# A hybrid attention and DeltaNet block: values in two half loads, and two delta heads' operands written in place

## The chip, the cores and the metric

The kernel runs on one core of a Trainium2 chip. The metric is the device time of one execution in microseconds (us), as a median over runs; every time in this document comes from such runs or from a profiled execution. Engines are named as the profile names them: PE is the matrix engine (TensorE), PEld its weight loads, DVE the vector engine, ACT the scalar engine, POOL the GpSimd engine, and SP the engine whose queue issues nearly all transfers of this kernel (SPq in the profile).

## The reference

One decoder block over 1024 tokens of width 1024, in float32. It normalises the input, projects it with one combined matrix, runs two groups of heads side by side, gates and normalises what they give, projects back, adds the input and normalises again:

```python
h = rmsnorm(x, norm1_w[layer])
proj = jnp.einsum('btd,de->bte', h, w_in[layer])
# stick-breaking attention: 8 heads of 64, query blocks of 128 rows over the causal keys
z = jnp.einsum('bhqd,bhkd->bhqk', qb, kb).astype(jnp.float32) * scale
sp = jnp.where(causal, jax.nn.softplus(z), 0.0)
tail = lax.cumsum(sp, axis=sp.ndim - 1, reverse=True) - sp
attn = jnp.where(causal, jnp.exp(jax.nn.log_sigmoid(z) - tail), 0.0)
outs.append(jnp.einsum('bhqk,bhkd->bhqd', attn.astype(v.dtype), vb))
# gated DeltaNet: 4 heads of 128, causal convolution of width 4 and silu on q, k, v, then
# chunks of tokens, a triangular solve in each, and a state carried from chunk to chunk
qkv = jax.nn.silu(causal_depthwise_conv(jnp.concatenate([g_q, g_k, g_v], axis=-1), gdn_conv_w[layer]))
v_new = u_c - jnp.einsum('bhcd,bhde->bhce', w_c, state)
o_c = jnp.einsum('bhcd,bhde->bhce', q_c * jnp.exp(g_c)[..., None], state) + jnp.einsum('bhij,bhje->bhie', a_c, v_new)
state = state * jnp.exp(g_last)[..., None, None] + jnp.einsum('bhcd,bhce->bhde', k_c * ..., v_new)
# both groups: rmsnorm per head, times silu of a gate, then
x = x + jnp.einsum('bte,ed->btd', mixed, w_out[layer])
return rmsnorm(x, final_norm_w)
```

## The kernel before, in words

Most products of the kernel are taken as three products of high and low parts (`mm3`), 128x512 at a time. The work on PE falls into three stretches. First the attention's queries and half of its values are projected. Then comes a long middle in which three kinds of work are interleaved: the remaining projections (`projections`, tile `pp`), attention (`attention`, `window`), and the delta heads (`delta_pre`, `delta_substitute`, `delta_solve`, `delta_scan`). The last stretch holds the products with the output matrix (`products_delta`, then `products_attention`; rows `pp<-wo` and `pp<-woh`), whose first factor `mm` is made for each block of 128 tokens from the heads' outputs and the gates.

The order of the work is not written down. While the program is built, a model of the engines (`Model`, `Recorder`) plays it through with costs written into the kernel: each stream is a generator, `interleave` takes the stream with the lowest number whose inputs are ready, and projections (number 100) fill PE when nothing else is ready. What the model found becomes the fixed order of every engine and of the SP queue. So an edit at one place can move instructions everywhere behind it. An engine or queue then keeps to its order: what stands first waits, and what is behind it waits with it. All instructions are recorded by one helper, which is why every row of the profile has the same line, and rows are told apart by their tiles.

**Attention.** A head's queries and keys (`q2`, `kh`, `kl`) are loaded from DRAM, and its values into `v2a`: 8 blocks of 128 tokens, 512 KB, one buffer. A head has four windows w of 256 queries. Each makes scores (`pz<-kh,q`, `pz<-kl,q`), passes them through ACT, DVE and POOL (`sg`, `cc`), transposes them (`pz<-step,st`), splits them (`ahl`), and multiplies the values with them (`po<-ahl,v2a`). In step j of window w the product reads blocks 2j-2 and 2j-1 of `v2a`. So blocks 4 to 7 are read in windows 2 and 3 alone, and blocks 0 to 3 for the last time in step 2 of window 3. `attention_values` loads the next head's values when the last window of the head before has ended (flag `e..3`); on the chip the load waits for the last product that reads the buffer.

**Delta heads.** `g_evac` turns a projected half (512 tokens) into q, k or v: convolution on ACT and DVE, then POOL multiplies `ac` by its sigmoid. For heads 0 and 1 (`TURNED` = 2) the result is stored to `g_s`, and `delta_load` loads keys and queries from there into `kq`, one of four slots, one for each unit (a head's half: head h, half g is unit 2h+g). Units 0 to 3 get the four slots; unit 4 waits for unit 0 to be done. `gdn_pre` transposes them (`pz<-step,kw`) and makes the triangular matrices (`pz<-kq`), `gdn_sub` and `gdn_inv` solve them, and `gdn_chain` carries the state through a unit's four chunks (`pc<-state,kq`, `pc<-xct,xinv`, `pz<-v,ak`, `pz<-state,kq`, `pz<-vr,ak`). At a unit's end the output is normalised, transposed and stored (`og_s<-akf`).

**The output's products** take blocks of 128 tokens in order, b = 0 to 7. Blocks 0 to 3 need unit 6 of the scan, blocks 4 to 7 unit 7; the first factor of a block goes into one of four slots `ak`, two of which units 6 and 7 hold until they are stored, so block 3 too waits for unit 7.

Of the kernel before, what the change touches and what calls it, by code (L numbers as in the profile page):

```python
# [134 lines left out]
class Fixed:  # L135
# [33 lines left out]
    def words(self, t, name):  # L169
        n = t.tensor.name  # L170
        return self.place(list(t.shape), F32R, name, self.at[n], self.ck.regions[n])


class Model:
# [304 lines left out]
def block(tc, xT_d, x_d, n1_d, wE_d, wQ_d, wC_d, conv_d, alog_d, dtb_d, mixw_d, wo_d, fnw_d, out_d):  # L479
# [4 lines left out]
    with ExitStack() as top:  # L484
# [139 lines left out]
        for tag, bufs in (("kh", 1), ("kl", 1), ("q2", 1), ("v2a", 1), ("sg2", 1), ("cc", 2), ("cc", 2), ("sg3", 1)):  # L624
            if tag[0] == "s":
                chl.append(fx.tile([P, 2, 520], F32R, "chl", tag))
            else:
                t = at_.tile([P, 1040 + (48 if tag == "kl" else 0)], F32R, tag=tag, bufs=bufs, name="chl")
                chl.append(t[:, 0:1040].rearrange("p (a e) -> p a e", a=2))
# [235 lines left out]
        def z_evac(i):  # L865
# [9 lines left out]

            return evac

        def g_evac(h, kind):
            wv = conv[:, 4 * kind + h, :]
            last = []  # L880

            def evac(pt, half):
                pre = gd.tile([P, 515], F32, tag="pre", bufs=2, name="pre")
                if half == 0:
                    V.memset(pre[:, 0:3], 0.0)
                else:
# [104 lines left out]
        def delta_load():  # L991
            yield lambda: "dec" in flags
            for h in range(GH):
                for g in range(2):
                    u = 2 * h + g
                    gst[h, g] = {}
                    half = "" if g else ".0"
                    yield lambda: u < 4 or f"c{u - 4}" in flags
                    if u > 3:
                        yield flags[f"c{u - 4}"]  # L1000
                    kq = fx.tile([P, 4, 2, P], F32, "kq", "kq")
                    ts = slice(512 * g, 512 * g + 512)
# [8 lines left out]
                    ck.hold(kq, kn, nkv)  # L1011
# [308 lines left out]
        def attention_values():  # L1320
            yield lambda: "v1" in flags and "dec" in flags
            for h in range(SBH):
                yield lambda: h == 0 or f"e{h - 1}3" in flags
                hd["v", h] = v2 = at_.tile([P, NB, P], F32R, tag="v2a", name="v2a")
                flags[f"va{h}"] = S.dma_start(v2.bitcast(F32), v_s[:, :, h].rearrange("b s u d -> s b (u d)").bitcast(F32))

        def window(h, w, tok):
            q2, kh, kl = hd[h]
# [29 lines left out]
            for j in range(w + 2):  # L1358
                if j <= w:
                    yield lambda: busy["al"] < 2  # L1360
                    busy["al"] += 1
                    blocks = [(s, i) for s in (2 * j, 2 * j + 1) for i in range(2) if s <= 2 * w + i]
                    n = len(blocks)
                    tp = pz()
                    yield from turned(tp, [st[:, i, s * P:(s + 1) * P] for s, i in blocks])
                    ahl = at_.tile([P, 2, 512], F32R, tag="ahl", bufs=2, name="ahl")
                    if n == 4:
                        halves = ahl.rearrange("p s (m t) -> p s m t", m=2)
                        ah, al = halves[:, :, 0, :], halves[:, :, 1, :]
                        src = tp.rearrange("p (s t) -> p s t", s=2)  # L1370
                    else:
                        ah, al = ahl[:, 0, 0:n * P], ahl[:, 1, 0:n * P]
                        src = tp[:, 0:n * P]
                    A.activation(ah, src, AF.Copy)
                    r = V.tensor_tensor(al, src, ah.bitcast(F32), ALU.subtract)
                    if j == w:
                        busy["T"] = 0
                        busy[tok] = 0
                    parts.append((ahl, r))
                    yield  # L1380
                if j == 0:
                    continue
                if j == 1:
                    yield lambda: busy["po"] == 0
                    busy["po"] = 1
                    ov = po()
                    yield from until(f"va{h}")
                    v2 = hd["v", h]
                ahl, r = parts[j - 1]
                ov2 = ov.rearrange("p (m t) -> p m t", m=2)  # L1390
                yield r
                for s in (2 * (j - 1), 2 * (j - 1) + 1):
                    i0 = 0 if s <= 2 * w else 1
                    c = slice(256 * (s % 2), 256 * (s % 2) + (1 if i0 else 2) * P)
                    if j <= w:
                        TE.matmul(ov, v2[:, s, :], ahl[:, s % 2, :], start=s == 0, stop=False)
                    else:
                        TE.matmul(ov2[:, :, i0 * P:256], v2[:, s, :], ahl[:, :, c], start=s == 0, stop=s == 2 * w + 1)
                busy["al"] -= 1
                if j < w + 1:  # L1400
                    yield
# [49 lines left out]
        def weight(k, wh, wl):  # L1451
            w = raws[k][0]
            A.activation(wh, w, AF.Copy, scale=mixw[:, k:k + 1])
            wts[k] = wh, wl, V.scalar_tensor_tensor(wl, w, mixw[:, k:k + 1], wh.bitcast(F32), ALU.mult, ALU.subtract)
            ck.free(w)

        def out_weights():
            places = [(t, 2 if t in ("cc", "ahl") else 1) for t in ("kh", "kl", "q2", "cc", "cc", "v2a", "ahl", "ahl")]
            for n, k in enumerate(range(4, 8)):
                yield lambda: k in raws and (n < 2 or f"e{SBH - 1}3" in flags)  # L1460
                yield raws[k][1]
                weight(k, *[at_.tile([P, D], F32R, tag=t, bufs=m, name="wo") for t, m in places[2 * n:2 * n + 2]])
                yield

        def out_weights_attention():
# [214 lines left out]
```

## Time and profile before

| | |
|---|---|
| median of 3 runs | 637.29 us (636.22 to 638.86) |
| the profiled execution: its own time | 639.53 us |
| its span, first to last instruction | 637.8 us |
| PE busy | 624.0 us (98%) |
| DVE, ACT, POOL busy | 447.5, 393.9, 341.2 us |
| mean granted clock of PE | 0.994 |
| bytes moved | 120.21 MB, 188 GB/s |

The profile has a page with sums, and views that answer questions about the trace: who waited for whom, instructions in order of time, and busy time in chosen stretches. Its times count from the first instruction. A row of a wait reads: engine, tile, line, what ended the wait, total us, times, longest. A row in order of time reads: start, duration, engine, line, operation, output<-inputs, shape, count, and in brackets the idle time ahead of it. In the stretches a number of us stands for each engine, then the granted clock, then the share of the transfer engines. Matmuls overlap: one of 128x512 lasts about 0.4 us, but the next starts long before it ends.

### The profile page before, as it was taken

The numbers are of one execution on the slowest core, as the hardware profiler recorded it, in microseconds if no ns is written. First come the engines' busy times: TensorE is split into PE (matmuls) and PEld (weight loads), VectorE is DVE, ScalarE is ACT, GpSimd is POOL, SyncE is SP. The second block draws the span as 40 slices with busy tenths as digits, with TensorE's granted clock in tenths as the row PEclk, the third lists the DMA queues.
The fourth block names the chain that finished last, engine by engine and source line by source line (L and its number), as shares of the span: only waits on it lengthen the run. The fifth ranks groups of instructions, "written<-read, shape, count | busy, mean of one in ns | idle before, by whom it ended". The sixth has DMA issues, their size and how long they took to land.

```text
span 637.8 us, 11259 instructions
## 1 busy us (share of the span) xinstructions
PE 624.0 (98%) x3672; PEld 528.7 (83%) x3672; DVE 447.5 (70%) x810; ACT 393.9 (62%) x945; POOL 341.2 (53%) x429
## 2 busy tenths in 40 slices
PE   8999999999999999999999989999999999999995
PEld 7889988988888888788888777888888888888884
DVE  4379973322797798887797696777889774478754
ACT  6665567724786776775785866666777653232553
POOL 0124047728794696881679684386764325245522
PEclk9999999999999999999999999899999999999998
DMA  8958337856557466598668768453652578984322
GB/s 305 342 183 312 124 131 253 303 189 222 159 151 224 131 185 134 141 207 221 167 146 224 185 133 264 121 185 94 180 141 84 151 201 255 311 319 143 116 100 100
DMA packets 165563, 120.21 MB, mean 188 GB/s; under 512 B 96448, under 2 KB 131456, under 8 KB 165504
## 3 DMA queue, kind: packets, MB, share of 16 engines
q1 hardware_dynamic: 165216, 119.29, 62.3%
q8 instruction: 29, 0.48, 0.3%
q14 instruction: 30, 0.25, 0.1%
q10 hardware_dynamic: 288, 0.20, 0.1%
HBM read 80.22 MB, written 39.23 MB: 187 GB/s over the span
## 4 chain that ended last, share of the span: by engine, by line
PE 81%; DMA 6%; ACT 4%; DVE 3%; SPq 2%; issue 2%; POOL 1%; POOLq 0%; DVEq 0%; ACTq 0%
PE pp L363 52%; PE pz L363 21%; PE po L363 6%; PE pc L363 3%; SPq L363 2%; DVE cc L363 1%; DMA v2a<-v_s 1%; DMA kh<-qk_s 1%; DMA xr1f<-xT 1%; DMA o_s<-oe 1%; ACT sgf L363 1%; POOL ac L363 1%; DMA qk_s<-sqh 1%; ACT pz L363 1%; DMA cb<-cum_s 1%
## 5 line engine op out<-in xcount | busy, mean ns | idle before, releaser
L363 PE MATMUL pp<-xh,weh 128*128 128x512 f32 x360 | 146.4, 407 | 0.4 <-DVE ac L363 0.4
L363 PE MATMUL pp<-xh,wel 128*128 128x512 f32 x360 | 141.8, 394 | 0.0
L363 PE MATMUL pp<-xl,weh 128*128 128x512 f32 x360 | 141.3, 392 | 0.0
L363 POOL TENSOR_TENSOR sgf<-sgf,cc 128x128 f32<-128x128 f32 (+3 forms) x64 | 77.5, 1216 | 57.7 <-DVE cc L363 52.5
L363 POOL TENSOR_TENSOR wel<-wer,weh 128x512 fp32r<-128x512 f32 x48 | 62.5, 1305 | 72.0 <-ACT weh L363 71.6
L363 PEld LDWEIGHTS pp<-xh,wel 128*128 128x128 f32 x360 | 68.0, 189 | 15.3
L363 PEld LDWEIGHTS pp<-xh,weh 128*128 128x128 f32 x360 | 68.1, 189 | 12.8 <-DVE ac L363 0.9
L363 PEld LDWEIGHTS pp<-xl,weh 128*128 128x128 f32 x360 | 68.1, 189 | 11.5
L363 DVE TENSOR_TENSOR_SCAN cc<-pz,step 128x384 f32<-128x384 f32 (+2 forms) x64 | 53.4, 844 | 10.6 <-ACT pz L363 9.5
L363 ACT ACTIVATE sgf<-pz,rs 128x384 f32<-128x384 f32 (+3 forms) x96 | 53.5, 593 | 7.6 <-PE pz L363 7.6
L363 DVE TENSOR_TENSOR ahl<-pz,ahl 128x512 fp32r<-128x512 f32 (+1 forms) x80 | 49.5, 630 | 12.0 <-ACT ahl L363 11.3
L363 ACT ACTIVATE ahl<-pz 128x512 fp32r<-128x512 f32 (+1 forms) x80 | 43.2, 559 | 20.6 <-PE pz L363 20.1
L363 ACT ACTIVATE pz<-pz,ns 128x384 f32<-128x384 f32 (+3 forms) x96 | 52.5, 576 | 0.0
L363 PE MATMUL po<-ahl,v2a 128*128 128x512 f32 (+1 forms) x160 | 48.9, 400 | 2.4 <-DMA v2a<-v_s 2.3
L363 PE MATMUL pp<-wo,mmf 128*128 128x512 f32 x192 | 45.5, 396 | 0.0
L363 DVE SCALAR_TENSOR_TENSOR pp<-pre,conv,pp 128x512 f32<-128x512 f32 x42 | 31.4, 747 | 18.2 <-ACT pp L363 17.8
L363 PEld LDWEIGHTS pp<-wo,mmf 128*128 128x128 f32 x192 | 35.8, 188 | 8.4
L363 PE MATMUL pp<-woh,mmf 128*128 128x512 f32 (+2 forms) x136 | 41.9, 385 | 0.0
L363 DVE TENSOR_TENSOR_SCAN cc<-pz,cc,step 128x512 f32<-128x512 f32 (+1 forms) x32 | 38.8, 1211 | 4.1 <-ACT pz L363 3.0
L363 POOL TENSOR_TENSOR mmf<-mgf,mmf 128x512 fp32r<-128x512 f32 x16 | 21.9, 1366 | 37.0 <-ACT mmf L363 23.9
L363 POOL TENSOR_TENSOR ac<-ac,pre 128x512 f32<-128x512 f32 x24 | 31.0, 1293 | 16.3 <-ACT pre L363 10.9
L363 DVE TENSOR_TENSOR xr<-pp,xr 128x512 f32<-128x512 f32 (+2 forms) x33 | 22.2, 672 | 23.0 <-PE pp L363 23.0
(317 smaller groups left out, 1513.9 us busy)
## 6 DMA issues: line engine op xcount, KB each, us to landing
wer<-wE SPq DMA_DIRECT2D x48, 256.0 KB, 3.5
xr<-x SPq DMA_DIRECT2D x16, 512.0 KB, 7.6
g_s<-ac SPq DMA_DIRECT2D x20, 256.0 KB, 2.3
v_s<-v2e SPq DMA_DIRECT2D x16, 256.0 KB, 3.3
kqf<-g_s SPq DMA_DIRECT2D x16, 256.0 KB, 4.0
v2a<-v_s SPq DMA_DIRECT2D x8, 512.0 KB, 5.9
q<-qk_s SPq DMA_DIRECT2D x8, 512.0 KB, 4.5
kh<-qk_s SPq DMA_DIRECT2D x8, 512.0 KB, 3.9
```

The costliest lines, as they stand in the source:

```text
L363: ins = f(*args, **kw).ins
```

## The change

Two edits. First, `v2a` becomes two buffers `v2ax` and `v2ay` of four blocks each (class `Two` makes them look like one to the early tile `chl` and to one output weight that use the same memory). The first half is loaded when step 2 of window 3 of the head before has been recorded (new flag `vx`), the second when that head has ended, as the whole was; a window waits for each half at its first step that reads it. Second, for heads 0 and 1 POOL's multiply writes keys and queries straight into the slot of `kq`, which `operand` now takes at the first such multiply; their 8 stores to `g_s` and 8 loads into `kq` are gone, and `delta_load` passes the multiply on as what to wait for. Values, and heads 2 and 3, are as before.

```diff
+class Two:
+    def __init__(self, *parts):
+        self.parts = parts
+    def __getitem__(self, ix):
+        if len(ix) == 3:
+            return self.parts[ix[1]][ix[0], ix[2]]
+        n = ix[1].start // 512
+        return self.parts[n][ix[0], ix[1].start - 512 * n:ix[1].stop - 512 * n]
...
+        operands = {}
+        def operand(h, g):
+            if (h, g) not in operands:
+                operands[h, g] = fx.tile([P, 4, 2, P], F32, "kq", "kq")
+                ck.hold(operands[h, g])
+            return operands[h, g]
...
+                ts = slice(half * 512, half * 512 + 512)
+                if h < TURNED and kind < 2:
+                    kq = operand(h, half)
+                    ck.prio, prio = BANK, ck.prio
+                    r = G.tensor_tensor(kq[:, :, 1 - kind, :], ac.rearrange("p (c t) -> p c t", c=4), sg.rearrange("p (c t) -> p c t", c=4), ALU.mult)
+                    ck.prio = prio
+                    return r
                 first(G.tensor_tensor, ac, ac, sg, ALU.mult)
-                ts = slice(half * 512, half * 512 + 512)
...
-                    kq = fx.tile([P, 4, 2, P], F32, "kq", "kq")
+                    kq = operand(h, g)
...
-                        loads.append(S.dma_start(kq[:, :, 1 - kind, :], g_s[h, kind, :, ts].rearrange("p (c t) -> p c t", c=4)))
+                        loads.append(flags[f"G{h}{kind}{half}"] if h < TURNED else S.dma_start(kq[:, :, 1 - kind, :], g_s[h, kind, :, ts].rearrange("p (c t) -> p c t", c=4)))
...
             for h in range(SBH):
-                yield lambda: h == 0 or f"e{h - 1}3" in flags
-                hd["v", h] = v2 = at_.tile([P, NB, P], F32R, tag="v2a", name="v2a")
-                flags[f"va{h}"] = S.dma_start(v2.bitcast(F32), v_s[:, :, h].rearrange("b s u d -> s b (u d)").bitcast(F32))
+                hd["v", h] = []
+                for n, c in enumerate("xy"):
+                    yield lambda: h == 0 or (f"e{h - 1}3" if n else f"vx{h - 1}") in flags
+                    v2 = at_.tile([P, 4, P], F32R, tag="v2a" + c, name="v2a")
+                    hd["v", h].append(v2)
+                    flags[f"va{h}{n}"] = S.dma_start(v2.bitcast(F32), v_s[4 * n:4 * n + 4, :, h].rearrange("b s u d -> s b (u d)").bitcast(F32))
...
-                    yield from until(f"va{h}")
-                    v2 = hd["v", h]
+                if j == 1 or j == 3:
+                    yield from until(f"va{h}{j // 2}")
...
+                v2 = hd["v", h][(j - 1) // 2]
...
+                if w == 3 and j == 2:
+                    flags[f"vx{h}"] = True
```

The change moves rows on every engine, from the first delta unit on. Three places matter to the prediction.

**The SP queue ahead of the load of head 4's values** (`xd`, `xe`, `xs`, `nb`, `xa`, `xb` belong to the delta heads' solve, `cb` and `dt` to `gdn_pre`, `o_s` and `og_s` are stores of outputs, `gt_s` of delta operands). Before:

```order
L363 DMA gt_s<-pre 32x16x32 x2
L363 DMA xd_100<-xs 32x16x16 x2
L363 DMA xe<-xs 64x128
L363 DMA wer<-wE 128x512 x2
L363 DMA vt<-gt_s 128x4x128
L363 DMA xs<-xd_99 128x1x128
L363 DMA nb<-bd 128x1x496
L363 DMA xa<-xd_100 128x1x128
L363 DMA xb<-xe 128x1x256
L363 DMA cb<-cum_s 128x512
L363 DMA dt<-dt_s 128x512
L363 DMA v2a<-v_s 128x8x128
```

Now:

```order
L376 DMA g_s<-ac 128x512
L376 DMA gt_s<-pre 32x16x32 x4
L376 DMA v2a<-v_s 128x4x128
L376 DMA o_s<-oe 32x8x32 x2
L376 DMA wer<-wE 128x512 x2
L376 DMA o_s<-oe 32x8x32
L376 DMA og_s<-akf_1809 32x16x32 x4
L376 DMA kqf_4406<-g_s 128x4x128 x2
L376 DMA nkv<-gt_s 128x4x128
L376 DMA xd_100<-xs 32x16x16 x2
L376 DMA xe<-xs 64x128
```

The first half now goes ahead of the solve's transfers that the whole stood behind.

**PE at the end of the delta scan** (`pc<-xct,xinv` and the rows `pz<-state` and `pz<-vr` are the last chunks of unit 7; `pp<-x` is a projection). Before:

```order
L363 MATMUL pc<-xct,xinv 128x128
L363 MATMUL pz<-state,kqf_4731 128x128
L363 MATMUL pz<-vr,akf_4734 128x128
L363 MATMUL pp<-xh,weh 128x512
L363 MATMUL pp<-xl,weh 128x512
L363 MATMUL pp<-xh,wel 128x512
L363 MATMUL pz<-state,kqf_4731 128x128
L363 MATMUL pz<-vr,akf_4734 128x128
```

Behind it stand 30 rows of projections before the first `pp<-wo`. Now:

```order
L376 MATMUL pc<-xct,xinv 128x128
L376 MATMUL pz<-state,kqf_4770 128x128
L376 MATMUL pz<-vr,akf_4773 128x128
L376 MATMUL pz<-state,kqf_4770 128x128
L376 MATMUL pz<-vr,akf_4773 128x128
L376 MATMUL pp<-wo,mmf_6693 128x512 x24
```

No projection is left behind the scan: the output's products follow it at once.

**The SP queue at the first delta units.** Before:

```order
L363 DMA wer<-wE 128x512 x2
L363 DMA g_s<-ac 128x512 x2
L363 DMA kqf_1074<-g_s 128x4x128
L363 DMA cum_s<-cs 32x2x128
L363 DMA dtf_1009<-cum_s 128x512
```

Now:

```order
L376 DMA wer<-wE 128x512 x2
L376 DMA cum_s<-cs 32x2x128
L376 DMA dtf_1009<-cum_s 128x512
L376 DMA dtf_1017<-cum_s 128x512
L376 DMA dt<-cum_s 128x512
```

The stores and the loads back are gone, and the decays' transfers move up by their places.

More of the change, by code (lines that the diff above doesn't have):

```diff
@@ L626, in block @@
                 chl.append(fx.tile([P, 2, 520], F32R, "chl", tag))
+            elif tag == "v2a":
+                chl.append(Two(*[at_.tile([P, 520], F32R, tag=tag + c, name="chl") for c in "xy"]))
             else:
@@ L1010, in delta_load @@
                     gst[h, g].update(kq=kq, kn=kn, nkv=nkv, at=at)
-                    ck.hold(kq, kn, nkv)
+                    ck.hold(kn, nkv)
                     turned = lambda kind: gt_s[h, kind, ts, :].rearrange("(c t) d -> t c d", t=P)
@@ L1395, in window @@
                     if j <= w:
-                        TE.matmul(ov, v2[:, s, :], ahl[:, s % 2, :], start=s == 0, stop=False)
+                        TE.matmul(ov, v2[:, s % 4, :], ahl[:, s % 2, :], start=s == 0, stop=False)
                     else:
-                        TE.matmul(ov2[:, :, i0 * P:256], v2[:, s, :], ahl[:, :, c], start=s == 0, stop=s == 2 * w + 1)
+                        TE.matmul(ov2[:, :, i0 * P:256], v2[:, s % 4, :], ahl[:, :, c], start=s == 0, stop=s == 2 * w + 1)
+                if w == 3 and j == 2:
+                    flags[f"vx{h}"] = True
                 busy["al"] -= 1
@@ L1453, in weight @@
             A.activation(wh, w, AF.Copy, scale=mixw[:, k:k + 1])
-            wts[k] = wh, wl, V.scalar_tensor_tensor(wl, w, mixw[:, k:k + 1], wh.bitcast(F32), ALU.mult, ALU.subtract)
+            for t, c in [(t, slice(512 * u, 512 * u + 512)) for u, t in enumerate(wl.parts)] if isinstance(wl, Two) else [(wl, slice(0, D))]:
+                r = V.scalar_tensor_tensor(t, w[:, c], mixw[:, k:k + 1], wh[:, c].bitcast(F32), ALU.mult, ALU.subtract)
+            wts[k] = wh, wl, r
             ck.free(w)
@@ L1461, in out_weights @@
                 yield raws[k][1]
-                weight(k, *[at_.tile([P, D], F32R, tag=t, bufs=m, name="wo") for t, m in places[2 * n:2 * n + 2]])
+                weight(k, *[Two(*[at_.tile([P, 512], F32R, tag=t + c, name="wo") for c in "xy"]) if t == "v2a" else at_.tile([P, D], F32R, tag=t, bufs=m, name="wo") for t, m in places[2 * n:2 * n + 2]])
                 yield
```

## Prediction

> **What bounds the kernel now.** I read the page's head first, then who waited on PE.
>
> ```profile
> span 637.8 us, 11259 instructions
> PE 624.0 (98%) x3672; PEld 528.7 (83%) x3672; DVE 447.5 (70%) x810; ACT 393.9 (62%) x945; POOL 341.2 (53%) x429
> ```
>
> ```profile
> engine line waited for: us in total, times, longest us
> PE po L363 <- DMA v2a<-v_s: 2.3, 1, 2.3
> PE po L363 <- DVE step L363: 1.7, 1, 1.7
> PE pz L363 <- ACT wy L363: 1.5, 1, 1.5
> PE pz L363 <- DVE cc L363: 0.6, 2, 0.4
> PE pp L363 <- DVE ac L363: 0.4, 1, 0.4
> PE pz L363 <- ACT nkv L363: 0.3, 1, 0.3
> PE pz L363 <- DVE state L363: 0.2, 1, 0.2
> ```
>
> PE bounds it, and nearly all its time is work: of 637.8 us it is idle for 13.8. Neither edit removes or adds a matmul (PE has the same operations in another order), so only idle time and a lowered clock can be won. 1.7 us is the wait for `step` at the start, which stays. The busy time by stretches shows the rest:
>
> ```profile
> core 0: us, PE busy (x) PEld busy (x) DVE busy (x) ACT busy (x) POOL busy (x), PEclk, DMA share, GB/s
> 366.60:369.00 2.40, 0.07 (x2) 0.04 (x1) 1.48 (x3) 1.44 (x5) 1.47 (x2) 1.00 1.12 303
> 396.60:398.10 1.50, 0.05 (x1) 0.05 (x1) 0.80 (x2) 1.27 (x3) 1.42 (x3) 1.00 0.70 197
> 398.60:402.10 3.50, 3.50 (x10) 2.72 (x9) 2.90 (x5) 3.46 (x10) 1.02 (x2) 0.51 0.94 254
> 631.20:637.80 6.60, 0.01 (x1) 0.00 (x0) 1.83 (x5) 0.61 (x1) 1.48 (x4) 0.72 0.36 143
> ```
>
> The last 6.6 us are the final block's normalisation and store, which the change doesn't touch. In the middle stand the wait for the values (2.3), the wait for `wy` (1.5), and right behind it a stretch at a granted clock of 0.51: 3.5 x (1 - 0.51) = 1.7 us lost. These three, 5.5 us, are most of what can be won.
>
> **Part one: values in halves.** The wait of 2.3 us is head 4's first use of its values. PE's last product for head 3 and the SP queue after it:
>
> ```profile
> 350.97 1.06 PE L363 MATMUL po<-ahl,v2a 128*128 128x512 f32 x4
> 368.96 0.62 PE L363 MATMUL po<-ahl,v2a 128*128 128x512 f32 x2 [2.33 <-DMA v2a<-v_s]
> ```
>
> ```profile
> 353.62 1.31 SPq L363 DMA_DIRECT2D xd<-xs  x2
> 354.98 1.48 SPq L363 DMA_DIRECT2D xe<-xs  x1
> 356.56 1.00 SPq L363 DMA_DIRECT2D wer<-wE  x2
> 361.34 0.43 SPq L363 DMA_DIRECT2D dt<-dt_s  x1
> 361.87 0.38 SPq L363 DMA_DIRECT2D v2a<-v_s  x1
> ```
>
> The buffer was free at 352.0, but its load was issued at 361.87: for 9.8 us the queue worked through what stood ahead of it. Now the load of the half that is needed first stands ahead of `xd` and `xe`, and its buffer is free four products sooner. I take the wait as gone: -2.3 (at the other end 0, if the half is late too). Sizes of transfers:
>
> ```profile
> kqf<-g_s SPq DMA_DIRECT2D x16, 256.0 KB, 4.0
> v2a<-v_s SPq DMA_DIRECT2D x8, 512.0 KB, 5.9
> g_s<-ac SPq DMA_DIRECT2D x20, 256.0 KB, 2.3
> ```
>
> A half (256 KB in rows of the same kind as `kqf<-g_s`) should land in about 4.0 us instead of 5.9.
>
> But the new order also starts the next head's products closer behind the old one's. One 128x512 product takes 0.23 us of PE, as the starts of two neighbours show:
>
> ```profile
> 361.16 0.40 PE L363 MATMUL pp<-xh,weh 128*128 128x512 f32 x1
> 361.39 0.39 PE L363 MATMUL pp<-xl,weh 128*128 128x512 f32 x1
> ```
>
> Between a first half's last reader and its first new use stand, for heads 6 and 7, 25 and 17 such products and some small ones: by rows some 8.5 us, of which 4.0 for the landing leaves 4.5 for the queue. Head 4's load lost 9.8 in the queue, and ahead of head 7's first half stand four `og_s` stores that wait for DVE. So a wait can come back here: 0 to 2.3 us, I take 0.5. The queue itself issues 8 transfers more here and 16 fewer in part two, each about 0.4 us as above: less work, none of it on PE's path.
>
> **Part two: delta operands in place.** Eight multiplies of POOL write four runs of 128 with a stride instead of 512 in a row. Both kinds are in the trace:
>
> ```profile
> L363 POOL TENSOR_TENSOR kqf<-kqf,cb x8: 1267/1288/1299, 120.9 to 406.1; 128x512 f32<-128x512 f32 x8
> L363 POOL TENSOR_TENSOR ac<-ac,pre x24: 1266/1294/1344, 87.4 to 363.6; 128x512 f32<-128x512 f32 x24
> ```
>
> 1288 against 1294 ns: nothing. The store and load that go are 2.3 + 4.0 = 6.3 us of latency for units 0 to 3. That is worth nothing by itself, since PE had projections to fill with; it moves the first transposes `pz<-step,kw` forward. The extra DVE operation for a split output weight is covered by DVE's idle 30%.
>
> **Part three: the reshuffled order.** The `wy` wait stood in a run of rows with no projection, between `pz<-wy` and `pz<-xinv` of head 2. In the new order that run is broken up by projections, so I take both the wait (-1.5) and the low clock behind it (-1.7) as gone; at the other end both come back elsewhere. The order holds new risks of the same kind: with two long waits in the old middle, I put one of 1.5 us into the new one (bounds 0 and the old 1.5 + 1.7).
>
> One lies open: the end. The scan's last matmul stood 30 projections ahead of the first output product, and now stands right ahead of it. The old end:
>
> ```profile
> 511.44 0.39 PE L363 MATMUL pz<-vr,akf 128*128 128x128 f32 x2
> 516.33 5.19 SPq L363 DMA_DIRECT2D og_s<-akf  x4
> 531.29 0.39 PE L363 MATMUL pz<-vr,akf 128*128 128x128 f32 x2
> 531.73 1.29 POOL L363 TENSOR_TENSOR mmf<-mgf,mmf 128x512 fp32r<-128x512 f32 x1 [2.65 <-ACT mmf L363]
> 538.37 9.90 PE L363 MATMUL pp<-wo,mmf 128*128 128x512 f32 x42
> 538.82 2.19 SPq L363 DMA_DIRECT2D og_s<-akf  x4
> 545.17 1.29 POOL L363 TENSOR_TENSOR mmf<-mgf,mmf 128x512 fp32r<-128x512 f32 x1 [7.85 <-DMA gate_s<-zt]
> 551.74 1.29 POOL L363 TENSOR_TENSOR mmf<-mgf,mmf 128x512 fp32r<-128x512 f32 x1 [5.28 <-DMA mgf<-gate_s]
> ```
>
> Unit 6 ended on PE at 511.44, and block 0's factor was ready at 531.73 + 1.29 = 533.0: a path of 21.6 us, with 26.9 to the first product. 29 fewer wide products now lie between, 29 x 0.23 = 6.7, so some 20.3 remain: 1.3 short, unless the stores (5.19 us here, 2.19 at unit 7) go faster, which gives back 3.0. Unit 7 ended at 531.29; block 3's factor was ready at 546.5 and block 4's at 553.0, paths of 15.2 and 21.7. A block has 24 products, 5.5 us, so block 3 was wanted at 538.37 + 16.5 = 554.9 and block 4 at 560.4: 8.4 and 7.4 us to spare. The new order takes about 7 of them. No reserve is left, but no debt either. Bounds 0 and 4.9 (unit 7's path as long as unit 6's 21.6, with block 3 wanted after 16.7); I take 1.0, nearer to the rows of unit 7 itself.
>
> **Sum.** -2.3 - 1.5 - 1.7 + 0.5 + 1.5 + 1.0 = -2.5 us. The profiled span 637.8 becomes 635.3. That execution took 639.5, 1.7 beyond its span; the median of the runs shown is 637.3, and I apply the same -2.5 to it: **634.8 us**, 0.4% less.
>
> The rows on the clock are worth weighing by themselves. A wait of 2.3 us at 366.6 left it at 1.00; one of 1.5 us at 396.6, behind many small matmuls, was followed by 3.5 us at 0.51. [...] If the low clock had nothing to do with the wait, it would stay, and the sum would be 636.5.
>
> **The rivals.** *All of it is won:* no new wait of size. For it: rows moved apart at both waits, and transfers taken off the queue; against it: heads 6 and 7, and the end. 637.3 - 5.5 = 631.8. *One for one:* every wait is replaced by one like it, since costs that set the order are not the chip's; 637.3. For it: nothing structural got shorter, and the delta chains of heads 2 and 3 stand later among PE's rows than before. This is also the case in which the change doesn't do what it says: halves wait in the queue as the whole did. *The delta scan bounds the end (slower):* unit 7's output is wanted 16.7 us after its last matmul and comes after 21.6: 4.9 us, and 1.7 more for a stretch at half clock. With the 2.3 of part one won and the `wy` pair back elsewhere: 637.3 - 2.3 + 6.6 = 641.6. It decides as soon as the waits at the products' start exceed what the middle wins by 3.2. Against it: no projections are left to crowd ACT, DVE and the queue there.
>
> **How the numbers follow.** A difference under 0.5%, 3.2 us, cannot be told from none: faster means below 634.1, slower above 640.5. The forecast has 0.43 (its own range 632.8 to 637), of which 0.12 lies below 634.1; all won 0.26; one for one 0.17, centred within; the scan at the end 0.14, nearly all above. Faster: 0.26 + 0.12 = 0.38. Same: 0.31 + 0.16 = 0.47. Slower: 0.14 + 0.01 = 0.15. The range, 630.8 to 640.6, takes in all won with 1 us to spare and the one-for-one case with the runs' own spread (1.6 above the median), and leaves out most of the case of the scan.
>
> **What would show it.** Right: no wait for `v2a` on PE above 0.5 us, no wait for `wy`, no stretch at 0.5 between 360 and 410; `pp<-wo` begins some 2 us earlier than 538.37, with at most a small wait for POOL's `mmf` there or at block 3 or 4. Part two right: `kqf<-ac,pre` about 1.29 us, 8 fewer `g_s` stores, PE unchanged by it. Wrong: a wait for `v2a` at head 6 or 7; idle PE between the blocks of `pp<-wo`; a low clock behind a wait at another place; or a PE sum that differs from 624, which would say that the order itself costs PE time.

## The result and the profile after

| | before | after |
|---|---|---|
| median | 638.08 us (636.22 to 640.95) | 646.76 us (643.59 to 647.56) |
| ratio of after to before | | 1.0135, 95% interval 1.0107 to 1.0163 |
| the profiled execution: its own time | 639.53 us | 646.23 us |
| its span | 637.8 us | 644.5 us |
| mean granted clock of PE | 0.994 | 0.991 |
| bytes moved | 120.21 MB | 116.01 MB |

The change made the kernel slower by 1.35%, 8.7 us, where 0.4% faster was forecast. The head of the page after, and who waited on PE:

```profile
span 644.5 us, 11242 instructions
PE 624.6 (97%) x3672; PEld 529.1 (82%) x3672; DVE 445.4 (69%) x811; ACT 394.1 (61%) x945; POOL 343.6 (53%) x429
PE pz L376 <- DVE cc L376: 5.7, 3, 5.4
PE pp L376 <- DVE xr L376: 2.9, 3, 1.7
PE po L376 <- DVE step L376: 1.7, 1, 1.7
PE pz L376 <- DVE dt L376: 0.7, 1, 0.7
PE pz L376 <- ACT vr L376: 0.6, 1, 0.6
PE pz L376 <- ACT pz L376: 0.4, 1, 0.4
PE pp L376 <- DVE v2e L376: 0.4, 1, 0.4
PE pz L376 <- DVE state L376: 0.2, 1, 0.2
```

PE does the same work (624.6 us busy, 624.0 before). The waits for `v2a` and for `wy` are gone, as forecast. In their place stand 5.7 us for `cc` and 2.9 for `xr`. All rows together are 12.6 us, against 7.0 before. The clock adds to it. Here is the stretch with the long wait, first in the kernel before, then in the changed one, then the part behind the wait by itself (columns: window, length, busy time of PE, PEld, DVE, ACT and POOL, granted clock, DMA share, GB/s):

```profile
256.00:272.00 16.00, 15.60 (x79) 12.78 (x79) 13.34 (x24) 12.75 (x43) 13.48 (x10) 1.00 0.61 134
```
```profile
256.00:272.00 16.00, 10.65 (x52) 8.94 (x51) 8.16 (x17) 7.15 (x19) 7.88 (x8) 0.79 0.81 207
266.30:270.20 3.90, 3.90 (x11) 3.17 (x12) 3.90 (x7) 1.56 (x6) 3.65 (x4) 0.50 0.90 205
362.00:412.00 50.00, 49.20 (x319) 41.03 (x318) 32.74 (x63) 35.70 (x108) 30.40 (x36) 1.00 0.82 221
```

In these 16 us PE is busy for 10.65 in place of 15.60. Behind the wait the clock is 0.50 for 3.9 us: 2.0 us lost to it, where before lost 1.7 behind its wait for `wy`. Waits +5.6 and clock +0.3 make +5.9; the spans differ by 6.7. The medians differ by 8.7: some 2 us of the loss are not in these two executions. The third row is the stretch that held both long waits before: PE is now busy there for all but 0.8 of 50 us, at full clock. So the gains came, and more was lost elsewhere.

**Where it was lost, first place.** Rows in order of time (start, duration, engine, operation, output<-input, and in brackets the idle time before and what ended it):

```profile
250.41 0.71 DVE L376 STREAM_TRANSPOSE pre<-ac 128x512 f32<-128x512 f32 x1
251.82 0.63 SPq L376 DMA_DIRECT2D xe<-xs  x1
255.74 1.79 SPq L376 DMA_DIRECT2D gt_s<-pre  x2
260.08 1.03 SPq L376 DMA_DIRECT2D gt_s<-pre  x2
265.13 0.06 DVE L376 MEMSET pre<- 128x3 f32 x1 [5.47 <-DMA gt_s<-pre]
266.30 0.60 PE L376 MATMUL pz<-step,stf 128*128 128x128 f32 x3 [5.35 <-DVE cc L376]
```

`pre`, the convolution's buffer (two of them), is written out to `gt_s` by four stores for delta heads 2 and 3. DVE had filled one at 251.1; SP issued the last of its stores at 260 to 261, because some ten other transfers stood ahead of them, and the last landed at 265.0. The next projected half needs that buffer. DVE's `MEMSET` of `pre` could start only then, after 5.47 us of idle time; the attention scans (`cc`) that stand behind it in DVE's order followed at 265.20, and PE waited 5.35 us for those.

**Second place: the end of the delta scan.**

```profile
540.18 0.49 PE L376 MATMUL pz<-vr,akf 128*128 128x128 f32 x2 [0.63 <-ACT vr L376]
545.60 0.69 DVE L376 TENSOR_TENSOR kqf<-kqf,norms 128x512 f32<-128x512 f32 x1 [3.82 <-POOL norms L376]
547.53 1.28 DVE L376 TENSOR_TENSOR xr<-pp,xr 128x512 f32<-128x512 f32 x2
548.35 11.85 PE L376 MATMUL pp<-wo,mmf 128*128 128x512 f32 x50 [1.68 <-DVE xr L376]
```

The scan's last matmuls are at 540.18, the output's products begin at 540.42 (538.37 before), and one bank of the products is not emptied in time: DVE first waits 3.82 us for the norms of the scan's last unit. Emptying a bank also adds the block's input `xr<-x`. Its first load was issued at 543.35 and landed at 546.55, 1 us before DVE came to it; before, it was issued at 535.56 and landed at 539.23.

The expectations below speak of the "loss" of a stretch. It is worked out from the trace: the distance between the starts of neighbouring rows on PE, less the median distance of that kind of matmul, summed. It holds waits and low clock alike. Its level shifts with the choice of what counts as one kind, by 1 or 2 us even in these stretches; the difference between two kernels in a stretch holds to about 0.5 us. Over the whole program it is 20.2 us before and 27.2 after; the difference, 7.0, answers the 6.7 of the spans. In 256 to 272 it is 1.1 before and 7.7 after, in 528 to 592 it is -0.8 and 3.9.

### The profile page after: what moved, and what is told of

It reads as the page before. It is cut to its first block, busy times and chain, and to the rows that moved or that the text cites. A ratio compares the mean times of both kernels' runs of the same rounds, so it can differ in the third digit from the quotient of the medians.

```text
span 644.5 us, 11242 instructions
## 1 busy us (share of the span) xinstructions
PE 624.6 (97%) x3672; PEld 529.1 (82%) x3672; DVE 445.4 (69%) x811; ACT 394.1 (61%) x945; POOL 343.6 (53%) x429
## 2 busy tenths in 40 slices
DMA packets 160314, 116.01 MB, mean 180 GB/s; under 512 B 96320, under 2 KB 127232, under 8 KB 160256
## 4 chain that ended last, share of the span: by engine, by line
PE 74%; DMA 6%; POOL 5%; issue 5%; DVE 4%; ACT 4%; SPq 1%; POOLq 0%; DVEq 0%; ACTq 0%
PE pp L376 43%; PE pz L376 21%; PE po L376 6%; PE pc L376 3%; DMA gt_s<-pre 2%; POOL mmf L376 1%; DMA q<-qk_s 1%; SPq L376 1%; DVE cc L376 1%; DMA og_s<-akf 1%; POOL oss L376 1%; ACT sgf L376 1%; ACT pre L376 1%; DMA gate_s<-zt 1%; DVE pp L376 1%
## 5 line engine op out<-in xcount | busy, mean ns | idle before, releaser
L376 PEld LDWEIGHTS pz<-step,stf 128*128 128x128 f32 x288 | 30.8, 141 | 11.6 <-issue 6.1
L376 PE MATMUL pz<-step,stf 128*128 128x128 f32 x288 | 34.4, 246 | 6.0 <-DVE cc L376 5.5
```

The lines of the kernel that those rows point to most:

```text
L376: ins = f(*args, **kw).ins
```

## The experiments

Three theories. **H**: two loads for one cost time themselves. **P**: operands written in place, and slots held early, cost time themselves. **O**: the operations cost nothing, and the loss is in the order that the planner found. Each ratio below is to the kernel before on the same chip, with its 95% interval.

### Each part alone

`half_only` is the change without the hunks on `operand`, `place_only` the change without those on `v2a`.

> Only the values in halves; keys and queries of heads 0 and 1 go through DRAM as before. In this order 48 projection matmuls stand between the delta scan's last matmul and the first output product (0 in the changed kernel, 30 before). Theory O (the loss is in the waits that the new order makes: stores late in the SP queue, and the scan at the very end): the end costs nothing here, no DVE wait of 5 us for a store of a convolution buffer unless this order makes one of its own; 632 to 639. Rival H (half loads cost by themselves, through the queue or the transfers): 641 to 647, with PE waits for v2a or behind it. Rival P (the operands in place cost by themselves): this is free of it, 632 to 636.

> Only the delta operands in place; values load whole. Here too 48 projections follow the scan's last matmul. Theory O: 632 to 640, with waits of its own order and no loss at the first output products. Rival P: 641 to 647, with the loss between 80 and 200 us, where the multiplies stand. Rival H: 632 to 636.

Measured: 648.88 us (1.0171, 1.0129 to 1.0214) and 645.66 us (1.0122, 1.0089 to 1.0156). Each part alone loses as much as both together, at places of its own: part one at 282 and 388 us (waits of 2.4 and 2.2 us for `ahl`), part two at 260 us (3.0 for `cc`) and 377 us (2.9 for `wel`). By their times alone the two runs look like theories H and P. What speaks against both is that costs of the operations would have added up, and these don't, and that between 80 and 200 us, where part two's multiplies stand, `place_only` loses no more than before (within 0.3 us).

### The stores of `pre` first

The order of after, with one conv buffer's four stores moved up on SP:

```diff
+move("S", "gt_s", "pre_2916", lambda o: o.out.startswith("o_s") and "oe_2962" in o.src)   # right behind xe
```

`stores_tail` also moves, at the end, POOL's last `norms` ahead of a product of `mmf` and DVE's first two emptyings of `pp` into `xr` ahead of the wait for `norms`.

> The changed kernel with one move in the SP queue: the four stores of one convolution buffer (gt_s<-pre of delta head 2, first half of v) go right behind the solve's store xe, ahead of o_s, akf, g_s, wer, xs and the half load of head 2's values, so about 3 to 5 us earlier; all other engines' orders are the same. Theory O: DVE's wait of 5.5 us for that buffer at 265 goes, with it PE's of 5.4 and the 3.5 us at half clock behind it: 7 us less, span 637 to 639, time 638 to 641. Rival (the wait is for something else that was late, or the stores land late whenever they are issued): under 2 us less.

> As stores_first, and two moves at the end of the delta scan: POOL does unit 7's normalisation ahead of the second block's factor, and DVE takes the first two output products out of PSUM ahead of unit 7's normalisation and transposition. Theory O for the end (PE waits 1.7 us at the first output products because DVE's evacuation stands behind unit 7's normalisation in its order, and the input block's load behind the pool that the scan frees): 1 to 2 us less than stores_first. Rival (the load of the input block lands too late whatever the order of DVE): no difference, and DVE then waits for the transfer xr<-x.

Measured: 644.57 us (1.0107, 1.0078 to 1.0137) and 645.33 us (1.0103, 1.0065 to 1.0141). The wait of 5.35 us fell to 0.50, so the place of these stores makes it. A wait of 2.40 us came up behind it at 271 us, and the loss in 256 to 288 us fell only from 9.0 to 5.9. By the ratios the kernel gained 1.8 us, not the 7 of theory O, and the two intervals overlap. At the end the second edit mended nothing: the wait for `xr` grew to 2.82 us, and DVE now waits for the transfer of the input block, as the rival in the expectation had it:

```profile
545.61 1.29 DVE L376 TENSOR_TENSOR xr<-pp,xr 128x512 f32<-128x512 f32 x2 [6.88 <-DMA xr<-x]
```

### Other orders for the same operations

The kernel before with one planner's constant changed (`SLACK = 430` for 450; `"S": 940` for 900 in `HOPS`):

> The kernel before with one constant of its planner changed, and nothing else: the slack that a stream of matmuls leaves after an operand is planned to be ready is 430 ns in place of 450. Every operation, tile and transfer is that of before; the planner's order differs (341 lines of difference on TensorE out of 2369 rows, 59 on SyncE, 63 on VectorE). Theory O (any new order loses the fit that the order of before has with the real queue times): slower than before by 3 to 10 us, with waits of TensorE on VectorE or ScalarE of 1 us and more at places that have nothing to do with attention's values or the delta heads' operands. Theories H and P (the half loads, or the operands in the slots, cost time themselves): within 2 us of before, 636 to 640 us, because nothing of either is in it.

> The kernel before with another single constant of the planner changed: the delay from the end of a transfer to its user is planned as 940 ns in place of 900. Operations, tiles and transfers are those of before; on TensorE 560 lines of difference, on SyncE 125, on VectorE 277, most of them behind row 2000 of TensorE. Theory O: slower than before by 3 to 10 us, the new waits in the stretch whose order differs. Theories H and P: 636 to 640 us.

Measured: 639.79 us (1.0038, 1.0014 to 1.0062) and 638.43 us (1.0016, 0.9993 to 1.0039). Against theory O as I had put it: a reordering alone costs 0 to 0.4%, not 0.5 to 1.6%. So not every new order is bad; those of the change, so far, were.

### The planner told of SP's queue

In the trace of before, the 609 transfers of SP signal on eight semaphores in turn, and no more than eight transfers are under way at any time. All 603 that follow another on the same semaphore (the two of ACT counted) start after its last signal, 30 of them less than 0.1 us after it. I read this as a limit: one is issued only when the one eight earlier has landed. The planner counts 475 ns for each issue and knows no such limit. This tells it:

```diff
+        self.lanes = [0.0] * 8
...
-            cost = 475
-            begin = max(self.now + 1100, self.dma)
+            cost = 475 + max(0.0, self.lanes.pop(0) - self.now)
+            begin = max(self.now + cost - 475 + 1100, self.dma)
             self.dma = begin + op.cost
+            self.lanes.append(self.dma + 1500)
```

> The changed kernel, with the planner told of a limit that the trace shows in SyncE's queue: a transfer is issued only when the one issued eight earlier has landed (so far the planner counts 475 ns for each issue, whatever is under way). Only the order differs, from the first row on. If the planner's wrong picture of SyncE's queue makes the new waits (5.35 us at 266 us, 1.7 at 548 us), the orders it now finds have fewer of them: 636 to 640 us, as before or better. If the waits come of any new order, whatever the planner knows of this queue: 642 to 650 us, with waits at other places.

> The kernel before with the same limit of SyncE's queue given to the planner, again from the first row on. If that picture was the fault: 632 to 638 us, not slower than before. If the order of before is a good one among many orders of like make, and a new one costs 3 to 10 us: 641 to 648 us. Beside the changed kernel with the same planner it also shows what the change is worth when neither order has been picked out: theories H and P want the changed kernel slower by 5 us and more, theory O wants the two within 4 us of each other.

Measured: 646.64 us (1.0136, 1.0105 to 1.0168) with the change, 635.34 us (0.9952, 0.9927 to 0.9977) without. The second is faster than both kernels of this case; its wait for head 4's values is 0.4 us. The first has nothing left at 256 to 272 us (loss 0.6) and 10.7 us in 528 to 592, most of it in this row, a wait of 1.44 us for POOL's `mmf` behind it, and the half clock, which began inside the first wait and lasted to 544.9 us:

```profile
539.08 1.22 PE L378 MATMUL pp<-wo,mmf 128*128 128x512 f32 x2 [5.75 <-ACT mmf L378]
```

So theories H and P still stood: with this planner the two kernels are 11 us apart, not the 4 that theory O allowed.

### The changed operations in the order of before

This tells operation from order. The planner reckons with the old operations, and the new ones are issued in their places. Part two: the sixteen transfers are planned and left out; POOL's instruction writes the slot.

```diff
+                if h < TURNED and kind < 2:
...
+                    real = nc.gpsimd.tensor_tensor(kq[:, :, 1 - kind, :], ac..., sg..., ALU.mult)
+                    first(planned, real.ins, ac, sg)              # planned as ac<-ac,sg
+                    return unissued(g_s[h, kind, :, ts], ac)      # planned, not issued; the loads likewise
```

Part one: one load is planned; two are issued, the first moved up on SP to where its four blocks are free.

> Part two of the change alone (keys and queries of the first two delta heads written into their slots by GpSimd, without the eight stores and eight loads), but every engine in exactly the order of the kernel before: the planner still reckons with the sixteen transfers, and they are only left out of SyncE's queue. So the operation is changed and the order is not. Theory O (the loss is in the new order alone): 636 to 639 us, as before. Theory P (GpSimd's write into the slots, or the slots held early, costs time itself): 642 us or more, as part two had with its own order (645.7).

> Part one alone (attention's values in two halves), with TensorE, ScalarE and GpSimd in exactly the order of the kernel before; on SyncE each first half stands where its blocks come free (3 to 17 places ahead of where the whole load stood), each second half where the whole load stood; VectorE splits one weight of the output in two instructions. Theory O: the wait of 2.3 us for head 4's values and the half clock behind it go and nothing comes in their place: 633 to 636 us. Theory H (two loads for one, or their places, cost time themselves): 640 us or more, as part one had with its own order (648.9).

> The whole change with the order of the kernel before: both edits of the two kernels beside it together. Theory O: 632.5 to 636 us, that is 10 us and more under the changed kernel with the order that its planner found, and faster than before by what the two waits and the half clock behind one of them are worth (2 to 4 us). Theories H and P: 642 us or more.

Measured: 639.76 us (1.0024, 1.0001 to 1.0048), 638.35 us (1.0006, 0.9985 to 1.0027) and 638.66 us (1.0025, 1.0006 to 1.0043). In all three traces PE's matmuls stand in exactly the order of before. Theories H and P fall as the cause of the loss: the whole change in the order of before costs 0.25% (0.43% at the interval's end), not 1.35%. The other half of theory O's expectation failed too, since nothing was gained. Waits on PE in `half_same`:

```profile
PE po L394 <- DVE step L394: 1.7, 1, 1.7
PE pz L394 <- DVE cc L394: 1.7, 3, 1.0
PE pz L394 <- ACT wy L394: 1.2, 1, 1.2
PE pp L394 <- DVE ac L394: 0.5, 1, 0.5
PE po L394 <- DVE ahl L394: 0.4, 1, 0.4
PE pz L394 <- ACT nkv L394: 0.3, 1, 0.3
PE pz L394 <- DVE dt L394: 0.3, 1, 0.3
```

The wait of 2.3 us for the values is gone, and `cc`, `ahl` and `dt` stand at 2.4 us together, against 0.6 for `cc` before: PE comes to the next steps sooner than DVE has made them. The rows sum to 6.1 us against 7.0.

### Another order for the change

> The changed kernel with the planner's slack at 430 ns in place of 450, as the kernel before had it in an earlier run (639.8 us there): another order for the same operations. If the order of the changed kernel was an unlucky draw: 636 to 642 us, as the other draws for the kernel before. If what the change lets the planner do (start head 4's values, the delta heads' units or the scan earlier) leads it to a worse order whatever the draw: 643 to 649 us.

Measured: 642.31 us (1.0066, 1.0039 to 1.0092), between the two expectations. The end of the scan costs nothing in this order (loss of -0.6 in 528 to 592), and the first place is the same and a little longer:

```profile
267.29 0.59 PE L376 MATMUL pz<-step,stf 128*128 128x128 f32 x3 [6.31 <-DVE cc L376]
```

### Is it the three large loads ahead?

In both orders of the change, and in that of part two alone, attention's `q`, `kh` and `kl` of a coming head (512 KB each) are issued at 238 us ahead of four small stores, which then take 5.3 us to issue. I took that for the cause.

```diff
+loads = [o for o in ops if o.out in ("q2_2871", "kh_2869", "kl_2870")]
...
+at = max(n for n, o in enumerate(rest) if o.out.startswith("gt_s") and "pre_2801" in o.src) + 1
+ck.order["S"] = rest[:at] + loads + rest[at:]
```

> The changed kernel with three rows of SyncE's queue moved: the loads of the second-next attention head's queries and keys (q, kh and kl, 512 KB each), issued at 237.9 to 239.7 us ahead of the four og_s stores, come behind the four gt_s stores that stood at 248 us. All else is the order of the changed kernel. Theory L (these 1.5 MB hold up the eight transfers that may be under way, og_s then takes 5.3 us to issue, the conv buffer's stores come late, VectorE waits for that buffer and TensorE for VectorE): the 5.35 us wait goes and the loss in 256 to 272 us falls from 7.7 us to under 2.5: 640 to 642.5 us, with the loss where the scan ends left. If the conv buffer's stores are late for another reason: 645 us or more. If the loads come too late where they stand now (first used at 256 us): a wait of TensorE on kl or q near 256 us in place of the other, 645 us or more.

> The same three rows moved in the changed kernel with the planner's slack at 430 ns, which had no loss where the scan ends and 8.3 us in 256 to 272 us (642.3 us). Theory L: 635 to 638 us, so that the wait behind the three loads and the end of the scan together are the whole loss of the change. If other losses of the new order remain: 639 us or more.

Measured: 648.55 us (1.0160, 1.0125 to 1.0195) and 641.58 us (1.0053, 1.0029 to 1.0077). The stores of `og_s` in the changed kernel, then in `loads_later`, with the wait of PE there:

```profile
241.89 5.34 SPq L376 DMA_DIRECT2D og_s<-akf  x4
```
```profile
241.64 1.94 SPq L376 DMA_DIRECT2D og_s<-akf  x4
266.60 0.60 PE L376 MATMUL pz<-step,stf 128*128 128x128 f32 x3 [5.81 <-DVE cc L376]
```

The stores of `og_s` were quick again, and the wait stayed: theory L falls. In `slack_loads` two stores `o_s` behind the loads took 2.47 us to issue instead, and the stores of `pre` were issued from 255.93 and 259.38 us, hardly earlier than without the move (255.9 and 260.9).

### The change in the good order

> The whole change in exactly the order that the kernel before has where its planner knows the limit of SyncE's queue (635.3 us): the sixteen transfers are planned and left out, the first halves of the values stand where their blocks come free. In that order the wait for head 4's values is 0.4 us, so the change has little left to win: 634 to 636.5 us. If the change were worth something of its own: under 633.5 us.

Measured: 636.33 us (0.9983, 0.9960 to 1.0006). The same order without the change had 0.9952 (0.9927 to 0.9977): the two differ by 0.31%, no more than the two intervals allow. It is again the change that is slower, as in the order of before (0.25%), so a cost of the operations of about that size is not excluded.

### Both places at once

`SLACK = 430`, and the stores of `pre` moved up as in `stores_first`:

> The changed kernel with the planner's slack at 430 ns (642.3 us: no loss where the scan ends, a wait of 6.3 us at 260 us) and, as in the earlier run with the kernel's own slack, the four gt_s stores of one conv buffer moved ahead in SyncE's queue, from 255.9 and 260.9 us to behind the store of xe at 251.7 us. Theory S (the place of these stores in SyncE's queue makes the wait, and this wait and the end of the scan are the loss): the wait falls under 1 us, the loss in 256 to 272 us from 8.3 to 4 us or less, and the time to 636.5 to 639.5 us, within 2 us of before. If the wait at 260 us is made elsewhere, or if clearing it only brings the next wait forward: 641 to 643 us.

Measured: 637.93 us (0.9994, 0.9979 to 1.0008). Against the same order without the move (1.0066), four stores' place on SP is worth 0.72%, 4.6 us. SP's row and the waits on PE:

```profile
252.16 2.47 SPq L376 DMA_DIRECT2D gt_s<-pre  x4
PE pz L376 <- ACT pz L376: 2.0, 1, 2.0
PE po L376 <- DVE step L376: 1.7, 1, 1.7
PE pp L376 <- DVE v2e L376: 0.4, 1, 0.4
PE pz L376 <- ACT wy L376: 0.4, 1, 0.4
PE pz L376 <- DVE cc L376: 0.3, 1, 0.3
```

Theory S holds. The wait for `cc` fell from 6.3 to 0.3 us, the loss in 256 to 272 us from 8.3 to 2.7 (a wait of 2.0 us took some of it back), and the change is level with before.

## Why the prediction was wrong

Term by term, against the profiled execution after:

| term of the sum | forecast | measured |
|---|---|---|
| wait for `v2a` | -2.3 | -2.3, no row of it left |
| wait for `wy` | -1.5 | -1.5, no row of it left |
| half clock at 398.6 to 402.1 | -1.7 | -1.7, clock 1.00 from 362 to 412 (perhaps luck, see below) |
| first halves late for heads 6 and 7 | +0.5 (0 to 2.3) | 0 |
| one new wait elsewhere | **+1.5 (0 to 3.2)** | **5.4 for `cc`, and 2.0 of half clock behind it: 7.4** |
| end of the scan | +1.0 (0 to 4.9) | 0.6 for `vr`, and 2.9 for `xr` (1.7 at 548 us, 1.2 at 580 and 587): 3.5 |
| POOL's write into the slots | 0 | 0: 1295 ns against 1294 |

The rows sum to +5.4, of the 6.7 between the two spans; the rest is in small rows. For the last row, the POOL rows of the changed kernel and the halves' landing (issues, KB, median us to landing):

```profile
L376 POOL TENSOR_TENSOR kqf<-ac,pre x8: 1271/1295/1302, 87.5 to 184.0; 128x512 f32<-128x512 f32 x8
v2a<-v_s SPq DMA_DIRECT2D x16, 256.0 KB, 3.4
```

**The step that failed** is in "Part three: the reshuffled order": "I put one of 1.5 us into the new one (bounds 0 and the old 1.5 + 1.7)". I sized the new order's waits by those of the order that was there. A wait in a new order isn't drawn from the waits of the old one: in the new one SP had the stores of `pre` behind some ten others, and the wait for that shared buffer lasted until the queue ahead of its release was through and the last store had landed, at 265.0 us (5.47 us on DVE, 5.35 on PE). The measured 7.4 us is more than twice the upper bound. Even all upper bounds of the sum together (-5.5 + 2.3 + 3.2 + 4.9) make +4.9, or 642.2 us. I had read SP's queue for `v2a` and for the end, but not for the buffers of which there are only two. The order of SP was known; `gt_s` behind `wer`, `xs` and `v2a` stood in it to be read.

**The end of the scan** was the right place with the right bounds, and sized low: 3.5 us in place of 1.0. I set "no reserve is left, but no debt either" from the factors `mmf`; what came late was `xr`, on DVE, whose queue waited 3.82 us for the norms of the scan's last unit, with the load `xr<-x` hardly earlier (546.55). I had followed neither.

**The -2.3 for the values** came true in the changed kernel, but it wasn't the change's to have: with the order kept, the wait goes and 0.9 us of 7.0 remain won, since other waits take its place. "I take the wait as gone" should have asked what PE would wait for next. The -1.5 came from the new order alone: `half_same`, with the old one, still waits 1.2 us for `wy`, and `before_lanes` waits 0.8 for it and 0.4 for the values without the change. The -1.7 can't be put down to the new order: the profiles of `place_same`, `half_same` and `both_same`, in the old order, have no half clock there either. Whether an execution shows it may be luck (last section).

**Part two's worth.** "That is worth nothing by itself, since PE had projections to fill with" is right as far as the operation goes (1.0024, interval from 1.0001). What I took for harmless, that it moves the delta heads' work forward, is what cost: all three orders in which the planner knew of it with its usual queue (`place_only`, after, `after_slack`) had the wait at 260 to 267 us, and neither reordering of before did.

**The rivals.** *The delta scan bounds the end* named one of the two places, at 641.6; alone, that place is worth about 4.4 us (1.0135 against 1.0066, though the two orders differ elsewhere as well). *One for one* had the mechanism that decided, "costs that set the order are not the chip's", and a price of zero for it. The true time lies beyond the range because two cases that I gave as alternatives came together.

**What stays open.** The two places account for 4.6 and 4.4 us of 8.7, each from a pair of runs, but only the first pair differs by nothing else, and it has the order of `SLACK = 430`: in the changed kernel's own order the same move was worth 1.8 us. Whether the operations themselves cost some 0.3% is open too. Why the planner leaves too little behind the scan in `after` and `after_lanes` (no projections between the scan's last matmul and the first output product; 27 to 48 in every other order that was planned) is argued from these orders and not tested: `place_only` has 48 and still loses 3.2 us in 528 to 592, on other tiles. The waits of `half_only` at 282 and 388 us were not followed to their source.

## What to carry to other kernels

When a change goes through a planner, split it: keep the old order by planning the old operations and issuing the new ones, and only then let the planner loose. That shows in one run whether a loss is in the work or in the order. For the blind sum, go through every buffer of which there are one or two and ask on which queue its release stands and behind what; here such a wait ended only with that queue and the landing, after 5.47 us on DVE, and PE, which needed what stood behind it on DVE, waited 5.35. And a planner's cost for a queue deserves measuring before the kernel is changed further: a few lines that told it of the eight transfers under way (the most in the trace of before) gained 0.48%, which no edit of the work did here.

## What the runs showed of the hardware

The clock behind a wait doesn't follow the wait's length alone: in before it stayed at 1.00 behind 2.33 us and fell to 0.50 behind 1.46 us. In the clock records of all 18 traces, the first full clock and every later change lie a whole number of steps of 3.41 us apart (from 6.07 to 398.61, 402.02 and 634.13 us in before, 115, 116 and 184 steps; 75, 77 and 185 in after), and the granted clock is 1.00 or 0.50 in between. The windows below are cut at these steps: four of the kernel before, two of `half_same`, two of `stores_first` (third column PE's busy time, the clock is the third number from the right):

```profile
364.47:367.88 3.41, 2.15 (x11) 1.30 (x9) 1.53 (x4) 2.67 (x11) 3.41 (x4) 1.00 0.99 283
367.88:371.30 3.42, 2.34 (x15) 2.08 (x16) 3.42 (x10) 1.43 (x4) 2.29 (x4) 1.00 0.95 224
395.19:398.61 3.42, 1.96 (x20) 1.70 (x19) 1.33 (x4) 2.75 (x11) 2.10 (x6) 1.00 0.61 182
398.61:402.02 3.41, 3.41 (x10) 2.63 (x9) 2.81 (x5) 3.41 (x10) 0.94 (x2) 0.50 0.94 254
```
```profile
395.42:398.83 3.41, 2.18 (x16) 1.78 (x14) 1.51 (x4) 2.92 (x10) 2.10 (x6) 1.00 0.76 175
398.83:402.24 3.41, 3.41 (x27) 2.72 (x26) 2.73 (x5) 2.79 (x8) 1.39 (x3) 1.00 1.12 284
```
```profile
270.41:273.82 3.41, 1.13 (x5) 0.56 (x3) 2.32 (x5) 3.41 (x16) 3.33 (x4) 1.00 0.81 181
273.82:277.24 3.42, 3.30 (x11) 2.99 (x12) 2.39 (x6) 3.07 (x11) 3.29 (x8) 0.50 0.41 108
```

In the kernel before, the wait of 2.33 us (366.62 to 368.95) is cut in two by a step, and each window keeps more than 2.1 us of busy PE: the clock stays. The wait of 1.46 us lies whole in one window, among small matmuls, with 1.96 us of busy PE: the next window has the half clock. The 1.23 us of `half_same` leave 2.18, and the clock stays. Over all 18 traces, 3269 windows at full clock, the 15 in which PE was busy for less than 1.6 us were each followed by the half clock. Of the 3246 above 2.15 us none was. Between 1.7 and 2.15 us two of eight were, so PE's busy time isn't quite what decides.

The second finding: executions of one kernel differ by their mean clock. Of the twelve of `half_same`, the five at 0.996 to 0.998 took 636.8 to 637.9 us, the seven at 0.991 to 0.994 took 638.3 to 639.7. One window at half clock costs 1.7 us and 0.0027 of the mean clock of a run of 637 us, by the row of before above. So the executions may differ by how many windows were caught, as the same waits fall otherwise between the steps; that is an estimate, for no slower execution of `half_same` was profiled. A profile is one such draw (that of `place_same` took 636.15 us against a median of 639.76): in this case medians of ten or twelve runs told apart what single profiles could not.
